# Branch B's scores: four products over 128 rows become six over 64 rows

## The chip, the cores and the metric

The kernel runs on one core of one Trainium2 chip. The metric is the device time of one execution in microseconds. The runs before the change took 1885.35, 1890.58 and 1890.80 us (median 1890.58). A profile is one execution, recorded instruction by instruction. Its engines are TensorE (PE; its weight loads are shown apart as PEld), VectorE (DVE), ScalarE (ACT), GpSimd (POOL) and SyncE (SP), which issues the DMA transfers.

## The reference

One layer of a bidirectional encoder is applied to 2048 prompt tokens and to 512 sample tokens, each with 16 learned meta tokens ahead. After a normalisation, one wide projection gives the operands of two attention branches, their gates, and two merge gates. Branch A is attention in a two-dimensional neighbourhood. Branch B, which the change touches, is attention in a sliding window:

```python
s_band = einsum('bnqkgd,bnckd->bnkgqc', qr, k_band) * scale + band_bias   # 128 queries, up to 3 blocks of 128 keys
s_band = where(visible, s_band, NEG_INF)
s_meta = einsum('bnqkgd,bmkd->bnkgqm', qr, km) * scale + meta_bias        # 16 meta keys
p = softmax(concatenate([s_band, s_meta, sink_col], -1), -1)
o = p[band] @ v_band + p[meta] @ v_meta
```

It has 8 query heads of width 64 and 2 key/value heads; four query heads share a key head. The branches' outputs are gated, projected, merged, projected again and added to the input, and a last normalisation follows. All inputs and outputs are 32-bit floats.

## The kernel before

The tokens are cut into 5 windows of 512 (`w`; window 0 is the sample). A first part computes all projections and writes queries, keys, values and gates to DRAM. A second part, from about 980 us on, runs the attention and the dense projections of the merge, window by window, first the units of branch A and then those of branch B.

**High and low parts.** TensorE takes its operands in a single-pass 32-bit type. To keep accuracy, an operand is split into a high part, rounded to that type, and a low part, the rest. A product of two split operands is made of part products.

**A unit of branch B** (`unit_b`) is one block of 128 queries (`n`, 4 in a window) for a pair of query heads (`p = 2 * gh + i`; `gh` is the key head). There are 5 x 2 x 4 x 2 = 80 units. Its keys are 18 columns of meta keys, sink and padding (`EXTRA`) and two or three blocks of 128, so a row of scores has 274 or 402 columns (`ncol`). The steps of a unit are:

1. load queries, keys, values, bias and gate (SP);
2. the scores of the two heads, each in a PSUM bank of the pool `ps_s`, which has two; VectorE adds the bias and takes the maximum (`scores_max`, L1042), ScalarE takes the exponential (`exps`, L1049);
3. normalise the probabilities;
4. transpose them on TensorE (L1237, L1240) and split them (L1244, L1245);
5. multiply with the values (L1261, L1264, L1266) and add into the output.

**Scores before.** A head is 64 wide and TensorE contracts over 128 rows. The tile of queries of a head has 128 rows: for each of the 64 features the high and the low part of the query, one below the other. The tile of keys `kbt` has the same 128 rows with the key's part repeated: once the high part in both rows, once the low part. So one product gives (high + low query) by high key, a second (L1218) adds (high + low query) by low key: all four part products in two products of 128 rows a head, four in a unit. To have the rows so arranged, the key is written to DRAM twice (`put_k`, one copy for each `j`) and read with feature and copy interleaved; the query is read with feature and part interleaved.

**The order of the work.** On TensorE the order is written out: the loop at the end of the attention steps through the units, with a unit's transposes while the next unit's scores are already made, and between the steps it calls `fill`, which issues pieces of the dense projections (L146, L147, L148: the three part products of `mm3`). In the projections SP's order is written out too; in the attention the order of SP, VectorE, ScalarE and GpSimd is set by a planner from its own cost estimates. A step waits on semaphores for its operands and for its buffers.

The lines that matter: L1217 and L1218 are the score products; L1111 and L1112 those of branch A; L185 and L361, early in the kernel, belong to the normalisation of the meta tokens (`spread` and `prep_last`) and work on 16 tokens: L185 has a product over 16 rows, L361 one with 16 columns; L142 is `move`, by which nearly all DMAs are issued.

Of the kernel before, what the change touches and what calls it, by code (L numbers as in the profile page):

```python
# [9 lines left out]
F32 = mybir.dt.float32  # L10
# [7 lines left out]
P = 128  # L18
D_MODEL = 1024
KT = D_MODEL // P  # L20
N_META = 16
# [3 lines left out]
TOK = SEQ + DEC_SEQ  # L25
WTOK = 512
# [6 lines left out]
EXTRA = N_META + 2  # L33
# [62 lines left out]
def encoder_block(ctx: ExitStack, tc: tile.TileContext, xT, x_end, w_in, w_pa, w_pb, w_o, norm_g, final_g,  # L96
                  final_row, bias_a0, bias_a1, bias_a2, bias_a3, bias_b, bias_b0, outT_p, outT_s, out_e):
    nc = tc.nc
# [4 lines left out]
    def dt(name, shape):  # L103
        return dram.tile(shape, F32, tag=name, name=name)

    qa_d = {(w, p): dt(f"qa{w}{p}", [P, 2, 2 * WTOK]) for w in range(NWIN) for p in range(4)}
    qb_d = {(w, p): dt(f"qb{w}{p}", [P, 2, WTOK]) for w in range(NWIN) for p in range(4)}
    ka_d = [dt(f"ka{p}", [P, 2, TOK]) for p in range(4)]
    kam_d = [dt(f"kam{p}", [P, 2, GRID_W]) for p in range(4)]
    kb_d = dt("kb", [P, 2, 2, TOK])  # L110
    kbm_d = dt("kbm", [P, 2, 2, EXTRA])
    va_d = [dt(f"va{p}", [2, TOK // GRID_W * 8, 8, P]) for p in range(4)]
    va0_d = [dt(f"va0{p}", [2, P, 6, P]) for p in range(4)]
    vrow_d = [dt(f"vrow{p}", [8, 8, 2, P]) for p in range(4)]
# [7 lines left out]
    def f32(ap):  # L122
        return ap.bitcast(F32)
# [17 lines left out]
    def move(out, in_):  # L141
        last_move[0] = nc.sync.dma_start(*(f32(a) if a.dtype == F32R else a for a in (out, in_)))  # L142
        return last_move[0]
# [73 lines left out]
    class Weights:  # L217
# [12 lines left out]
        def split(self, i):  # L230
            if i < len(self.srcs):
                self.wt[i] = split_w(self.raw.pop(i))
# [377 lines left out]
    def put_k(br, w, p, src):  # L610
        e = ev.tile([P, 2, WTOK], F32R, tag="ev", name="evk")
        split(e[:, 0, :], e[:, 1, :], src, 0.125)
        ws = slice(w * WTOK, (w + 1) * WTOK)
        if br == "a":
            move(ka_d[p][:, :, ws], e)
        else:
            for j in range(2):
                move(kb_d[:, j, :, ws], e)

    km = st.tile([P, 2, GRID_W], F32R, tag="km", name="km", bufs=1)  # L620

    def put_k_meta(br, p, src):
        c0, n = (META_COLS[0], len(META_COLS)) if br == "a" else (0, 1)
        if p == 0:
            nc.vector.memset(f32(km), 0.0)
        hi, lo = (km[:, i, c0 : c0 + n * N_META].rearrange("p (n m) -> p n m", m=N_META) for i in range(2))
        split(hi, lo, src[:, None, :].broadcast_to([P, n, N_META]), 0.125)
        if br == "a":
            move(kam_d[p], km)
        else:  # L630
            for j in range(2):
                move(kbm_d[:, j], km[:, :, :EXTRA])

    def transposed(dst, src, nch, n):

# [97 lines left out]
    def put_kv(f, w, src):  # L733
        if f < VA:
            put_k("a", w, f - KA, src)
        elif f < ZA:
            put_values("a", w, f - VA, src)
        elif f == KB:
            put_k("b", w, 0, src)
        else:  # L740
            put_values("b", w, 0, src)
# [23 lines left out]
    def alone(f, wt, held):  # L765
# [27 lines left out]
        if f in (*range(KA, VA), KB):  # L793
            put_k_meta(br, p, tm)
        else:
            later(lag[0], put_v_meta, br, p, tm)
# [242 lines left out]
    def scores_max(s, n, bias):  # L1039

        nm = at.tile([P, 1], F32, tag="nm", name="nm", bufs=8)
        nc.vector.tensor_tensor_reduce(s[:, :n], s[:, :n], bias, -1.0, 3.0e38, ALU.add, ALU.min, nm)  # L1042
        return nm

    def sums_of():
        return at.tile([P, 2], F32, tag="sm", name="sm", bufs=8)

    def exps(out, s, nm, sm):
        nc.scalar.activation(out, s, AF.Exp, bias=nm, scale=-1.0, accum_out=sm)  # L1049
# [115 lines left out]
    def unit_b(w, gh, n, i, sh):  # L1165
# [1 line left out]
        kinds = [b_blocks(w, m) for m in range(4)]  # L1167
        tlo = kinds[0][0]
        thi = kinds[3][0] + kinds[3][1] * P
        gs = slice(64 * gh, 64 * gh + 64)  # L1170
        p = 2 * gh + i
        b0, nbk, first = kinds[n]
        ncol = EXTRA + nbk * P
        qs = slice(n * P, (n + 1) * P)
# [3 lines left out]
        if n == 0 and i == 0:  # L1178
            q = sh["q"] = ld.tile([P, 2, 2, WTOK], F32R, tag="q", name="q")
            for j in range(2):  # L1180
                move(q[:, j], qb_d[w, p + j].rearrange("(h d) i t -> (d i) h t", h=2))
            bt = sh["b"] = ld.tile([P, 2, 2, EXTRA + 3 * P + N_META], F32, tag="ba", name="bb")
            for j in range(2):
                move(bt[:, j, :, : EXTRA + 3 * P], bias_b[p + j])
                move(bt[:, j, 0, EXTRA + 3 * P :], bias_b[p + j][:, 0, :N_META])
# [6 lines left out]
            move(z, z_d["b", w, p])  # L1192
        if i == 0:
            kt = sh["k"] = ld.tile([P, 2, EXTRA + 3 * P + N_META], F32R, tag="kd", name="kbt")
            move(kt[:, :, EXTRA : EXTRA + nbk * P],
                 kb_d[gs].rearrange("d j i t -> (d j) i t")[:, :, b0 : b0 + nbk * P])
            move(kt[:, :, :EXTRA], kbm_d[gs].rearrange("d j i t -> (d j) i t"))
            move(kt[:, :, ncol : ncol + N_META], kbm_d[gs].rearrange("d j i t -> (d j) i t")[:, :, :N_META])
        kt, q, z = sh["k"], sh["q"][:, i], sh.get(("z", i))
        yield  # L1200
        if n == 0:
# [6 lines left out]
        if nbk == 2 and not first:  # L1208
            nc.vector.tensor_copy(bt[:, 0, ncol : ncol + N_META], bt[:, 0, :N_META])
        sm = sums_of()  # L1210
        for h in range(2):
            if h and (gh, n, i) == (0, 0, 0):
                yield
            s = ps_s.tile([P, WTOK], F32, tag="s", name="s")

            ks = slice(N_META * (1 - h), N_META * (1 - h) + ncol)
            nc.tensor.matmul(s[:, :ncol], q[:, h, qs], kt[:, 0, ks], start=True, stop=False)  # L1217
            nc.tensor.matmul(s[:, :ncol], q[:, h, qs], kt[:, 1, ks], start=False, stop=True)  # L1218
            nm = scores_max(s, ncol, bt[:, h, ks])
            exps(prs[:, cols[h]], s[:, :ncol], nm, sm[:, h : h + 1])  # L1220
        yield
# [37 lines left out]
        for m, (j, hi, lo) in enumerate(parts):  # L1259
            vb = sh["v"][:, (b0 - tlo) // P + j, :]  # L1260
            nc.tensor.matmul(o[:, : 2 * P], vb, hi, start=(m == 0), stop=False, skip_group_check=True)  # L1261
            if m == nbk - 1:
                for h in range(2):
                    nc.tensor.matmul(o[:64, h * P : (h + 1) * P], vms[:, gh, h, :], pms[(2 * n + i) % 2], start=False,  # L1264
                                     stop=False, skip_group_check=True)
# [3 lines left out]
        for h in range(2):  # L1269
            hs = slice(64 * h, 64 * h + 64)  # L1270
# [232 lines left out]
    for w in range(NWIN):  # L1503
        for p in range(4):
            sh = {}
            units += [("a", w, unit_a(w, p, h, g, sh), 1) for h in range(2) for g in range(4)]
        for gh in range(2):
            sh = {}
            units += [("b", w, unit_b(w, gh, n, i, sh), 2) for n in range(4) for i in range(2)]
# [13 lines left out]
    ps_s = ctx.enter_context(tc.tile_pool(name="ps_s", bufs=2, space=PSUM))  # L1523
# [10 lines left out]
    with tc.manual_schedule(engines={E.PE}):  # L1534
# [22 lines left out]
        for i in range(N):  # L1557
            br, w, _, weight = units[i]
# [128 lines left out]
```

## Time and profile before

| | |
|---|---|
| runs, median (lowest to highest) | 1890.58 us (1885.35 to 1890.80) |
| profiled span, first to last instruction | 1881.7 us |
| median of the runs less the span | 8.9 us |
| TensorE busy | 1855.9 us, 9797 products, as many weight loads |
| VectorE, ScalarE, GpSimd busy | 1320.6, 1145.5, 730.0 us |
| mean granted TensorE clock | 0.999 |
| DMA, mean rate | 226 GB/s |
| branch B's score products | 320: 256 of 402 columns, 64 of 274 |

The profiled execution's own time outside the profiler is not known; beside its span of 1881.7 us stand the runs. In a row of the timeline the numbers are start and duration in us, then the engine, the line of the kernel, the operation, the tile written and the tiles read, and the shape: `128*64 128x256` is a product over 128 rows with 64 stationary columns and 256 moving ones. Products are pipelined, so the duration of one is longer than the distance to the next. In a row of the groups stand the busy time, the mean duration in ns, and the idle time before with what ended it.

### The profile page before, as it was taken

Reading aid. Unit: us, or ns where it says so; the run is one execution under the profiler, and the core shown is the slowest. Engines: PE = TensorE matmul, PEld = TensorE weight load, DVE = VectorE, ACT = ScalarE, POOL = GpSimd, SP = SyncE. Lnnn points to the kernel's source line nnn. Section 1 sums busy time; section 2 is a strip of 40 time slices with the busy share of each in tenths; the row PEclk is TensorE's granted clock in tenths of the full one; section 3 lists DMA queues with packets and bytes.
Section 4 is the critical chain, followed back from the end, with each engine's and each line's share of the span. In section 5 each row is a group of like instructions: output and inputs, shape, how many; then the busy total and the mean of one; then the engine's idle time right before and its main releaser. Section 6 shows DMA issues by size and latency. Waiting matters only on the chain. (4 is left out here: it accounts for less than half of the span.)

```text
span 1881.7 us, 29782 instructions
## 1 busy us (share of the span) xinstructions
PE 1855.9 (99%) x9797; PEld 1583.0 (84%) x9797; DVE 1320.6 (70%) x2961; ACT 1145.5 (61%) x2528; POOL 730.0 (39%) x558
## 2 busy tenths in 40 slices
PE   8999999999999999999999999999999999999998
PEld 6898888888888888888888888888888888888887
DVE  8886657556477565444457888878787887888874
ACT  6454444444365443444456797797789788878932
POOL 2005443323202233322324435656744763685420
PEclk9999999999999999999999999999999999999999
DMA  7667756544296777744258878977985996798383
GB/s 268 234 175 295 207 171 193 211 175 179 84 348 219 235 216 200 209 138 161 104 197 310 273 217 266 304 213 249 316 280 179 320 315 225 222 311 260 119 299 135
DMA packets 290385, 424.83 MB, mean 226 GB/s; under 512 B 117416, under 2 KB 162040, under 8 KB 288696
## 3 DMA queue, kind: packets, MB, share of 16 engines
q1 hardware_dynamic: 289944, 422.93, 69.5%
q8 instruction: 78, 1.28, 0.3%
q14 instruction: 75, 0.61, 0.1%
q10 hardware_dynamic: 288, 0.01, 0.0%
HBM read 303.46 MB, written 119.39 MB: 225 GB/s over the span
## 5 line engine op out<-in xcount | busy, mean ns | idle before, releaser
L208 POOL TENSOR_TENSOR wt<-wraw,wt 128x512 fp32r<-128x512 f32 x164 | 213.1, 1318 | 265.9 <-ACT wt L207 265.8
L848 PE MATMUL pa<-u,wt 128*128 128x512 f32 x1008 | 242.5, 389 | 0.0
L848 PE MATMUL pa<-u,x 128*128 128x512 f32 x984 | 236.9, 390 | 1.2 <-ACT u L859 1.1
L207 ACT CAST wt<-wraw 128x512 fp32r<-128x512 f32 x312 | 177.9, 619 | 74.8 <-PE mm L148 35.3
L848 PEld LDWEIGHTS pa<-u,wt 128*128 128x128 f32 x1008 | 189.0, 188 | 39.2
L848 PEld LDWEIGHTS pa<-u,x 128*128 128x128 f32 x984 | 184.3, 188 | 40.6 <-ACT u L859 2.2
L819 POOL TENSOR_TENSOR s<-wraw,raw 128x512 f32<-128x512 f32 x40 | 58.3, 1458 | 265.5 <-DVE x L208 265.5
L146 PE MATMUL mm<-u,wt 128*128 128x512 f32 (+2 forms) x416 | 150.4, 362 | 7.8 <-ACT u L334 7.2
L814 POOL TENSOR_TENSOR s<-raw 128x512 f32<-128x512 f32 x40 | 58.3, 1456 | 250.0 <-DMA raw<-in_w_in_dram 245.0
L148 PE MATMUL mm<-u,wt 128*128 128x512 f32 (+2 forms) x416 | 146.6, 352 | 2.4 <-DVE wt L208 2.4
L147 PE MATMUL mm<-u,wt 128*128 128x512 f32 (+2 forms) x416 | 146.6, 352 | 1.3 <-DVE u L335 1.3
L208 DVE TENSOR_TENSOR wt<-wraw,wt 128x512 fp32r<-128x512 f32 x148 | 107.2, 762 | 47.2 <-ACT wt L207 47.0
L848 PE MATMUL pe<-u,wt 128*128 128x512 f32 x504 | 121.3, 390 | 0.0
L848 PE MATMUL pc<-u,wt 128*128 128x512 f32 x504 | 121.1, 389 | 0.0
L848 PE MATMUL pe<-u,x 128*128 128x512 f32 x480 | 115.3, 389 | 0.0
L848 PEld LDWEIGHTS pc<-u,wt 128*128 128x128 f32 x504 | 94.6, 188 | 19.6
L848 PEld LDWEIGHTS pe<-u,wt 128*128 128x128 f32 x504 | 94.4, 188 | 19.6
L1139 DVE TENSOR_TENSOR pl<-tp,ph 128x384 fp32r<-128x384 f32 (+6 forms) x160 | 94.8, 593 | 20.2 <-ACT ph L1138 17.7
L1138 ACT CAST ph<-tp 128x384 fp32r<-128x384 f32 (+6 forms) x160 | 81.7, 510 | 43.4 <-PE tp L1135 41.9
L146 PE MATMUL pso<-mh,wt 128*128 128x512 f32 x256 | 107.1, 418 | 0.0
L827 POOL TENSOR_TENSOR s<-wraw,s 128x512 f32<-128x512 f32 x40 | 55.4, 1384 | 131.6 <-DVE wt L208 126.3
L848 PEld LDWEIGHTS pe<-u,x 128*128 128x128 f32 x480 | 90.1, 188 | 18.7
(258 smaller groups left out, 5017.0 us busy)
## 6 DMA issues: line engine op xcount, KB each, us to landing
wraw<-in_w_in_dram SPq DMA_DIRECT2D x86, 512.0 KB
qa<-evq SPq DMA_DIRECT2D x20, 1024.0 KB
raw<-in_w_in_dram SPq DMA_DIRECT2D x40, 512.0 KB
q<-qa SPq DMA_DIRECT2D x20, 1024.0 KB
wraw<-in_w_o_dram SPq DMA_DIRECT2D x32, 512.0 KB
kbt<-kb SPq DMA_DIRECT2D x32, 384.0 KB
qb<-evq SPq DMA_DIRECT2D x20, 512.0 KB
ka<-evk SPq DMA_DIRECT2D x20, 512.0 KB
```

The costliest lines, as they stand in the source:

```text
L146: nc.tensor.matmul(ps, wh, uh, start=first, stop=False)
L147: nc.tensor.matmul(ps, wh, ul, start=False, stop=False)
L148: nc.tensor.matmul(ps, wl, uh, start=False, stop=last)
L207: nc.scalar.copy(h, r)
L208: low[0] = (eng or lo_eng[0]).tensor_sub(l, r, f32(h)).ins
L814: eng.tensor_add(s1, a21, a22)
L819: eng.tensor_sub(s3, a11, a21)
L827: eng.tensor_sub(s4, a12, s2)
L848: nc.tensor.matmul(ps, wt[:, a, s], u[:, b, kk, :], start=first and kk == 0 and i == 0, stop=kk == 3 and i == 2, skip_group_check=True)
L1138: nc.scalar.copy(ph_[:kb, a], tb)
L1139: nc.vector.tensor_sub(pl_[:kb, a], tb, f32(ph_[:kb, a]))
```

## The change

Head 0 of a pair takes rows 0 to 63 of TensorE's array, head 1 rows 64 to 127. The query tile's 128 rows are now the two heads' 64 features; its high and low parts lie side by side along the free axis (`q[hs, iq, qs]`). The key tile has the same key head in both halves, its high and low part side by side (`kt[hs, ik, ...]`). For each head there are three products of 64 rows: high query by high key, high by low, low by high; the product of the two low parts is dropped. The two heads' products alternate, and both score banks are taken before the first. The keys are written to DRAM into a tensor for each key head, into both halves of its 128 rows, with four transfers where there were two (the meta keys likewise); queries and keys are read back without interleaving.

```diff
-    kb_d = dt("kb", [P, 2, 2, TOK])
-    kbm_d = dt("kbm", [P, 2, 2, EXTRA])
+    kb_d = [dt(f"kb{g}", [P, 2, TOK]) for g in range(2)]
+    kbm_d = [dt(f"kbm{g}", [P, 2, EXTRA]) for g in range(2)]
...
-            for j in range(2):
-                move(kb_d[:, j, :, ws], e)
+            for g, j in (0, 0), (0, 1), (1, 0), (1, 1):
+                move(kb_d[g][64 * j : 64 * j + 64, :, ws], e[64 * g : 64 * g + 64])
...
-            for j in range(2):
-                move(kbm_d[:, j], km[:, :, :EXTRA])
+            for g, j in (0, 0), (0, 1), (1, 0), (1, 1):
+                move(kbm_d[g][64 * j : 64 * j + 64], km[64 * g : 64 * g + 64, :, :EXTRA])
...
-                move(q[:, j], qb_d[w, p + j].rearrange("(h d) i t -> (d i) h t", h=2))
+                move(q[:, j], qb_d[w, p + j])
...
-            move(kt[:, :, EXTRA : EXTRA + nbk * P],
-                 kb_d[gs].rearrange("d j i t -> (d j) i t")[:, :, b0 : b0 + nbk * P])
-            move(kt[:, :, :EXTRA], kbm_d[gs].rearrange("d j i t -> (d j) i t"))
-            move(kt[:, :, ncol : ncol + N_META], kbm_d[gs].rearrange("d j i t -> (d j) i t")[:, :, :N_META])
+            move(kt[:, :, EXTRA : ncol], kb_d[gh][:, :, b0 : b0 + nbk * P])
+            move(kt[:, :, :EXTRA], kbm_d[gh])
+            move(kt[:, :, ncol : ncol + N_META], kbm_d[gh][:, :, :N_META])
...
         sm = sums_of()
+        kss = [slice(N_META * (1 - h), N_META * (1 - h) + ncol) for h in range(2)]
+        ss = [ps_s.tile([P, WTOK], F32, tag="s", name="s") for _ in range(2)]
+        for m, (iq, ik) in enumerate(((0, 0), (0, 1), (1, 0))):
+            for h in range(2):
+                hs = slice(64 * h, 64 * h + 64)
+                nc.tensor.matmul(ss[h][:, :ncol], q[hs, iq, qs], kt[hs, ik, kss[h]], start=m == 0, stop=m == 2)
+        if (gh, n, i) == (0, 0, 0):
+            yield
         for h in range(2):
-            if h and (gh, n, i) == (0, 0, 0):
-                yield
-            s = ps_s.tile([P, WTOK], F32, tag="s", name="s")
-
-            ks = slice(N_META * (1 - h), N_META * (1 - h) + ncol)
-            nc.tensor.matmul(s[:, :ncol], q[:, h, qs], kt[:, 0, ks], start=True, stop=False)
-            nc.tensor.matmul(s[:, :ncol], q[:, h, qs], kt[:, 1, ks], start=False, stop=True)
+            s, ks = ss[h], kss[h]
             nm = scores_max(s, ncol, bt[:, h, ks])
             exps(prs[:, cols[h]], s[:, :ncol], nm, sm[:, h : h + 1])
```

More of the change, by code (lines that the diff above doesn't have):

```diff
@@ L1169, in unit_b @@
         thi = kinds[3][0] + kinds[3][1] * P
-        gs = slice(64 * gh, 64 * gh + 64)
         p = 2 * gh + i
```

## The prediction

> **What bounds the kernel now.** I read the page first (busy time, slices), then the busy time by stage, then TensorE's timeline around a unit of branch B.
>
> ```profile
> PE 1855.9 (99%) x9797; PEld 1583.0 (84%) x9797; DVE 1320.6 (70%) x2961; ACT 1145.5 (61%) x2528; POOL 730.0 (39%) x558
> ...
> PE   8999999999999999999999999999999999999998
> ...
> 1380.00:1460.00 80.00, 79.71 (x485) 70.72 (x484) 65.39 (x194) 72.21 (x186) 37.63 (x29) 1.00 0.67 210
> 1460.00:1540.00 80.00, 79.44 (x482) 68.81 (x481) 64.85 (x166) 61.18 (x139) 60.33 (x48) 1.00 1.01 317
> ```
>
> The last two rows are two 80 us stages: the first holds the 16 B units of a window, the second A units. The columns are PE, PEld, DVE, ACT, POOL, then the granted clock (1.00), the DMA share and GB/s. TensorE has 0.29 us without work in a whole B stage; ACT is next with 72.21 of 80. A busy PE may still be PE waiting inside its pipeline, so the test is the spacing of its products (timeline: start, duration, engine, line):
>
> ```profile
> 1398.22 0.28 PE L1264 MATMUL ob<-pms,vms 96*64 96x128 f32 x2
> 1398.34 0.28 PE L1266 MATMUL ob<-pl,vb 128*64 128x256 f32 x1
> 1398.46 0.35 PE L1217 MATMUL s<-kbt,q 128*128 128x402 f32 x1
> 1398.64 0.34 PE L1218 MATMUL s<-kbt,q 128*128 128x402 f32 x1
> 1398.83 0.35 PE L1217 MATMUL s<-kbt,q 128*128 128x402 f32 x1
> 1399.01 0.35 PE L1218 MATMUL s<-kbt,q 128*128 128x402 f32 x1
> 1399.20 0.39 PE L146 MATMUL pso<-mh,wt 128*128 128x512 f32 x1
> 1399.42 0.39 PE L147 MATMUL pso<-ml,wt 128*128 128x512 f32 x1
> ```
>
> A duration (0.35 us) is a product's passage through the array; the price is the distance between starts. The unit's four score products take 1399.20 - 1398.46 = 0.74 us, 0.185 us each, and 512 columns take about 0.23 us: both near 2.2 columns a nanosecond, with no gap on either side. So TensorE's stream sets the end here, and what the change adds to or takes from this stream is worth its full length. Units with 274 columns:
>
> ```profile
> 1783.38 0.29 PE L1217 MATMUL s<-kbt,q 128*128 128x274 f32 x1
> 1783.51 0.30 PE L1218 MATMUL s<-kbt,q 128*128 128x274 f32 x1
> 1783.64 0.29 PE L1217 MATMUL s<-kbt,q 128*128 128x274 f32 x1
> 1783.77 0.29 PE L1218 MATMUL s<-kbt,q 128*128 128x274 f32 x1
> 1783.90 0.39 PE L146 MATMUL psa<-ya,wt 128*128 128x512 f32 x1
> ...
> L1217 PE MATMUL s<-kbt,q 128*128 128x402 f32 x128 | 44.6, 348 | 0.0
> L1217 PE MATMUL s<-kbt,q 128*128 128x274 f32 x32 | 9.3, 301 | 0.6 <-ACT prs L1049 0.6
> ```
>
> Here a product costs 0.52 / 4 = 0.13 us. L1217 runs twice a unit, so 128 / 2 = 64 units have 402 columns and 16 have 274: 80 units.
>
> **The change, part by part.**
>
> *The products.* Four products of 128 rows become six of 64 rows: for each of three parts (high by high, high by low, low by high; low by low is dropped), head 0 in rows 0 to 63 and head 1 in rows 64 to 127, into two PSUM banks. No row of this trace has two products on disjoint rows; every product shares rows with its neighbour, and they stream one after the other. So the cost has two ends. If the two heads of a part stream together, a unit takes three rounds: 3 x 0.185 = 0.555 us, 0.185 us less than now (0.13 us less at 274 columns): 64 x 0.185 + 16 x 0.13 = 13.9 us gained. If they stream one after the other, it takes six: 2 x 0.185 = 0.37 us more (0.26 at 274): 64 x 0.37 + 16 x 0.26 = 27.8 us lost. I take the first end: what makes neighbours queue in every row above is that they want the same rows of the array, and these two share neither rows nor bank.
>
> The Trainium skill, "TensorE: Matmul & The Clock Gate", Part 3 (packing small matmuls), says that products on distinct row groups run concurrently, and gives 3.07 times for four of 32 rows; no run here shows it. By it the products alone would gain the 13.9 us.
>
> *Stagger.* Six weight loads replace four. A load of the second head queues behind the first's; the two 96-row products of L1264 lie (1398.34 - 1398.22) / 2 = 0.06 us apart, loads included. So head 1 starts up to 0.06 us after head 0 and ends as much later: 0 to 0.06 us a unit, and I take 0.06, since a load cannot be skipped. Later loads have a round of 0.185 us for two, and hide.
>
> *Switching the array's division.* Before and after each unit's scores TensorE runs products over 128 rows. Weight loads (PEld) normally start far ahead. Two places early in the kernel show what a switch to fewer rows or columns does, and back:
>
> ```profile
> 22.86 0.70 PE L360 MATMUL fin_v<-ones,rs 128*128 128x1 f32 x5
> 23.49 0.11 PEld L361 LDWEIGHTS fin_v<-ones,rs 128*16 128x16 f32 x2
> 23.49 0.20 PE L361 MATMUL fin_v<-ones,rs 128*16 128x1 f32 x2
> 23.62 0.19 PEld L146 LDWEIGHTS mm<-u,wt 128*128 128x128 f32 x1
> ...
> 31.54 0.29 PEld L185 LDWEIGHTS rs_rb<-rs_dg,ones 16*128 16x128 f32 x2
> 31.54 0.39 PE L185 MATMUL rs_rb<-rs_dg,ones 16*128 16x16 f32 x2
> 31.86 0.19 PEld L146 LDWEIGHTS mm<-u,wt 128*128 128x128 f32 x1
> 31.86 0.50 PE L146 MATMUL mm<-u,wt 128*128 128x512 f32 x1
> 32.20 0.40 PE L147 MATMUL mm<-u,wt 128*128 128x512 f32 x1
> ```
>
> The 16-row products end at 31.54 + 0.39 = 31.93, and the load of the next, 128-row product starts only at 31.86, 0.07 us before. The same 0.07 us stands at 23.49 (before 22.86 + 0.70 = 23.56) and at 23.62 (before 23.69): the load waits until the array is nearly empty. The product behind it ends at 32.36, 0.43 us after the one before, where 512 columns normally end 0.23 us after (L147 ends at 32.60): a switch costs 0.20 us. Against it stand 64-column products:
>
> ```profile
> 1398.28 0.14 PEld L1266 LDWEIGHTS ob<-pl,vb 128*64 128x64 f32 x1
> 1398.34 0.19 PEld L1217 LDWEIGHTS s<-kbt,q 128*128 128x128 f32 x1
> ...
> L1266 PE MATMUL ob<-pl,vb 128*64 128x256 f32 x224 | 60.0, 281 | 0.0
> ```
>
> L1266's product runs from 1398.34 to 1398.62, and the load of the 128-column product after it starts at 1398.34, 0.28 us before that end: no emptying. So a switch costs between 0 (64 columns) and 0.20 us (16 rows, 16 columns). For 64 rows I take 0.20: the change divides the rows, and the one row-divided place, on the way out, pays it in full. Two switches a unit: 0.40 us, 80 x 0.40 = 32.0 us.
>
> The Trainium skill, "TensorEngine Tiling (Array Packing)", Key Properties, says that changing the tiling mode, not just the tile, drains the array. The trace agrees at 16 rows and columns and shows no drain at 64 columns; by the rule without exception the switches cost the 32.0 us, by the 64-column row nothing.
>
> *Order within the unit.* Both score banks must now be free before the second product, not before the third, and head 0's scores are complete later. The chain behind the scores of 1398.46, and the next unit's:
>
> ```profile
> 1399.02 0.58 DVE L1042 CUSTOM_DVE_ANT_0 s<-s,bb 128x402 f32<-128x402 f32 x1 [0.53 <-PE s L1218]
> 1401.80 0.59 ACT L1049 ACTIVATE prs<-s,nm 128x402 f32<-128x402 f32 x1
> 1403.55 0.35 PE L1217 MATMUL s<-kbt,q 128*128 128x402 f32 x1
> ```
>
> Head 0's maximum starts at 1399.02; head 1's exponential, which frees the second bank, ends at 1401.80 + 0.59 = 1402.39, and the next scores start at 1403.55. The second bank was needed two products later, 1.5 us after that end; now 1.16 us. Head 0's scores come some 0.2 to 0.6 us later, and this slack hides it: 0. Without that cover each unit would wait for ACT, as once already (0.6 us, in the row of L1217 above). Behind a waiting score product stands the dense fill; there is no other new wait.
>
> *DMAs.* Keys go out in four transfers a window instead of two (10 more in all), the meta keys in four instead of two; loads keep their number and bytes, a query row becoming one run instead of two.
>
> ```profile
> L142 SPq DMA_DIRECT2D kb<-evk x10: 382/456/472, 127.1 to 758.3; - x10
> ```
>
> Twelve issues of 0.456 us are 5.5 us of SP spread over the projections; the keys written last at 758.3 are read by B units after 1060. Hidden: 0.
>
> *Sum.* At 402 columns: -0.185 + 0.06 + 0.40 = +0.275 us; at 274: -0.13 + 0.06 + 0.40 = +0.33 us. 64 x 0.275 + 16 x 0.33 = 17.6 + 5.3 = 22.9 us longer. The profiled span is 1881.7 us, so 1904.6 us; the median of the runs, 1890.58 us, lies 8.9 us above the span (the runs spread by 5.5 us), which gives **1913.5 us**.
>
> **The rivals.**
>
> *Pairs together, switches free* (the other side). The array runs 64-row tiles as it runs 64-column ones: loads go ahead, three rounds follow with no gap. Place: the two edges of each unit's scores. Price: -13.9 us to -13.9 + 80 x 0.06 = -9.1 us; 1876.7 to 1881.5, about 1878 us. For it: every row of size 64 in the trace, and these are of the same number type as the scores; against it: the 16-row rows, the only ones with divided rows. It decides as soon as a switch costs less than (13.9 - 4.8) / 160 = 0.057 us.
>
> *One after the other.* The heads don't overlap. With free switches +27.8 us: 1918.4 us; with drained ones +27.8 + 32.0 = +59.8 us: 1950 us. For it: no two products in the trace overlap in the array. Against it: none could have. This is also the case in which the change does not do what it says.
>
> *A cheaper switch.* If a switch costs about half (0.10 us), the sum is -9.1 + 16.0 = +6.9 us without other luck, and about +2 us with no stagger: 1893 to 1898 us. For it: nothing but the middle between the two bounds.
>
> *ACT takes over.* In the B stage ACT is busy 72.21 of 80 us; with 2.2 to 2.8 us less of TensorE per stage it would reach 93%. It would blunt the gain of the first rival, not turn it; I count it in its range.
>
> **How the numbers follow.** Together and drained (forecast, 1913): 0.42, its own range 1906 to 1917. Together and free (1878): 0.36, range 1876 to 1883. In series, free (1918): 0.08. In series and drained (1950): 0.07. Cheaper switch (1893 to 1898): 0.07. About 0.3% (5.7 us) is what a measurement of this kernel tells from no change. Faster: 0.36 and a little of the last, 0.37; same: 0.06; slower: 0.42 + 0.08 + 0.07, 0.57. The range must reach from the free case to the drained one: 1876 to 1919; it leaves out the fully drained series.
>
> **What would show it.** The number of TensorE products rises by 160 to 9957 in every case. Together: the two heads' products of one part start less than 0.1 us apart and parts 0.185 us apart; in series: six starts 0.185 us apart. Drained: the first weight load of a unit's scores, and the first load after them, start 0.07 us before the end of the product before; free: 0.28 us or more before. The stage of 16 B units lengthens by 16 x 0.275 = 4.4 us if I am right, and shortens by 2 to 3 us if the first rival is. I am wrong if loads at the switch run ahead as in L1266, or if the time moves outside the B stages by more than 3 us.

## The result and the profile after

The kernel after takes 1919.18 us (median of 4 runs, 1918.28 to 1921.56) against 1889.49 us before (one more run of the kernel before, of 1888.40 us, has moved its median). The ratio is 1.0169, 95% interval 1.0152 to 1.0185: slower by 28.7 to 35.0 us. The forecast was slower, at about 1913 us in a range of 1876 to 1919; the time lies 0.2 us above the range and 6 us above the forecast. The span of after's profile lies 1.9 us below its own execution's time (1919.7 against 1921.56). By that, some 7 of the 8.9 us that the prediction put around the span of 1881.7 us mean that its profile was of a quick execution.

First the switch and the pairs. The timeline of TensorE in one unit after (start, duration, engine, line):

```profile
1422.64 0.28 PE L1266 MATMUL ob<-pl,vb 128*64 128x256 f32 x1
1422.86 0.82 PE L1214 MATMUL s<-kbt,q 64*128 64x402 f32 x6
1423.61 0.50 PE L146 MATMUL pso<-mh,wt 128*128 128x512 f32 x1
```

Its weight loads in the same stretch:

```profile
1422.86 0.48 PEld L1214 LDWEIGHTS s<-kbt,q 64*128 64x128 f32 x6
1423.61 0.19 PEld L146 LDWEIGHTS pso<-mh,wt 128*128 128x128 f32 x1 [0.27 <-issue]
```

Six products of 402 columns are through in 0.82 us: one passage of 0.45 us and two more rounds of 0.185 us. Six in a row would need five more, 1.37 us. The ends of products are modelled in the trace, but the starts are recorded, and L146 starts 0.75 us after the first of the six, which is less than six rounds of 0.185 us (1.11 us). So the pairs stream together. The first score load starts at 1422.86, 0.06 us before the end of L1266 (1422.64 + 0.28 = 1422.92); the load after the scores starts at 1423.61, 0.07 us before the scores' end (1422.86 + 0.82 = 1423.68). At both edges the load waits until the array is nearly empty, as at the 16-row place of before.

From the end of the product before the scores to the end of the 512-column product after them it is 1423.61 + 0.50 - 1422.92 = 1.19 us here; before, 1399.20 + 0.39 - (1398.34 + 0.28) = 0.97 us. Over all units with such neighbours the medians of this distance, taken from the product ends in the trace, are 0.964 us before and 1.178 us after at 402 columns, 0.746 and 1.012 us at 274. That gives 64 x 0.214 + 16 x 0.266 = 18.0 us.

The second part of the loss lies ahead of the first changed product. The weight loads of branch A's first score product, grouped by line, first before and then after (behind the count the shortest, median and longest in ns, then the starts of the first and the last):

```profile
L1111 PEld LDWEIGHTS s<-kd,q x160: 186/188/192, 981.5 to 1712.2; 128*128 128x128 f32 x160
```

```profile
L1111 PEld LDWEIGHTS s<-kd,q x160: 186/188/330, 991.0 to 1746.7; 128*128 128x128 f32 x160
```

The projections end 9.5 us later, before any 64-row product has run. The issues of the key stores on SP after, in a row of the same form:

```profile
L142 SPq DMA_DIRECT2D kb<-evk x20: 514/644/1243, 129.5 to 769.2; - x20
```

The median issue takes 0.644 us (0.456 before), and there are twice as many: over the five windows the key stores hold SP for 15.0 us where it was 4.4. Among TensorE's waits after in the first 981 us, this is the row for ScalarE's copies (sum, number, longest):

```profile
PE pa L848 <- ACT u L859: 5.1, 4, 2.3
```

TensorE stood four times for them, 5.1 us in all.

Third, the clock. Busy time by stage after, the columns as in the prediction (PE, PEld, DVE, ACT, POOL, granted clock, DMA share, GB/s):

```profile
1294.00:1298.00 4.00, 2.75 (x19) 2.19 (x17) 3.92 (x12) 3.75 (x10) 1.62 (x2) 1.00 0.69 194
1298.40:1301.60 3.20, 3.20 (x10) 2.63 (x11) 2.46 (x13) 1.12 (x4) 0.00 (x0) 0.50 0.59 195
1302.00:1306.00 4.00, 4.00 (x27) 3.14 (x26) 3.20 (x13) 2.29 (x7) 0.07 (x1) 1.00 0.02 6
```

And TensorE's timeline at the beginning of the second row:

```profile
1297.37 1.02 PE L170 MATMUL fin_v<-ones,ssq 128*128 128x1 f32 x8 [1.25 <-DVE pms L1255]
1298.25 0.73 PE L146 MATMUL psa<-ya,wt 128*128 128x512 f32 x1
1298.78 0.63 PE L147 MATMUL psa<-ya,wt 128*128 128x512 f32 x1
```

After TensorE stood for 1.25 us, the granted clock is 0.50 for some 3.4 us, and products of 512 columns pass in 0.63 us instead of 0.39. Half speed for 3.4 us costs about 1.7 us, an estimate. The profile of after shows three such stretches in the attention (from 1298.3, 1380.2 and 1649.9); the profile of before shows none there, nor does the second profile of before below. The other two come behind stands of 2.07 us (at 1379.0) and 1.05 us (at 1647.6). But a stand of 1.05 us at 1474.9 has none behind it, nor has one of 1.82 us in the second profile of before, so the length of one stand alone does not decide it.

The Trainium skill, "TensorE: Matmul & The Clock Gate", gives windows of some 3.4 us, and half rate after at least one idle window (section "What's actually happening"). Half rate and length agree with these rows; the idle window does not, since the stands ahead of the three stretches were shorter, 1.05 to 2.07 us.

### The profile page after: what moved, and what is told of

Its sections match the earlier page's. It is cut to its first block, busy times and chain, and to the rows that moved or that the text cites. A ratio compares the mean times of both kernels' runs of the same rounds, so it can differ in the third digit from the quotient of the medians.

```text
span 1919.7 us, 30120 instructions
## 1 busy us (share of the span) xinstructions
PE 1883.1 (98%) x9957; PEld 1573.8 (82%) x9957; DVE 1323.2 (69%) x2961; ACT 1142.6 (60%) x2528; POOL 725.5 (38%) x558
## 3 DMA queue, kind: packets, MB, share of 16 engines
q8 instruction: 79, 1.29, 0.3%
## 4 chain that ended last, share of the span: by engine, by line
PE 46%; ACT 5%; DMA 4%; DVE 3%; issue 1%; POOL 0%; SPq 0%; DVEq 0%; ACTq 0%
PE pa L848 6%; PE pe L848 3%; PE tp L1135 3%; PE pso L146 2%; PE pso L148 2%; PE pso L147 2%; PE s L1214 2%; DMA sgb<-gb 2%; PE psa L146 2%; PE tp L1237 2%; PE psa L148 2%; PE pc L848 2%; PE psa L147 2%; PE psb L148 2%; PE psb L147 1%; PE psb L146 1%
## 5 line engine op out<-in xcount | busy, mean ns | idle before, releaser
L848 PE MATMUL pa<-u,wt 128*128 128x512 f32 x1008 | 243.1, 390 | 0.6 <-ACT s L859 0.4
L848 PE MATMUL pa<-u,x 128*128 128x512 f32 x984 | 237.2, 390 | 5.1 <-ACT u L859 5.1
L848 PEld LDWEIGHTS pa<-u,wt 128*128 128x128 f32 x1008 | 188.7, 188 | 41.0 <-ACT s L859 0.8
L848 PEld LDWEIGHTS pa<-u,x 128*128 128x128 f32 x984 | 184.3, 188 | 45.1 <-ACT u L859 6.8
L146 PE MATMUL mm<-u,wt 128*128 128x512 f32 (+2 forms) x416 | 151.8, 365 | 7.8 <-ACT u L334 7.2
L848 PE MATMUL pe<-u,wt 128*128 128x512 f32 x504 | 121.3, 390 | 0.0
L848 PE MATMUL pc<-u,wt 128*128 128x512 f32 x504 | 121.1, 389 | 0.0
L848 PE MATMUL pe<-u,x 128*128 128x512 f32 x480 | 115.3, 389 | 0.0
L1049 ACT ACTIVATE prs<-s,nm 128x402 f32<-128x402 f32 (+1 forms) x160 | 90.9, 571 | 40.7 <-DVE nm L1042 39.8
L146 PE MATMUL pso<-mh,wt 128*128 128x512 f32 x256 | 112.4, 439 | 0.0
L848 PEld LDWEIGHTS pc<-u,wt 128*128 128x128 f32 x504 | 94.6, 188 | 19.6
L848 PEld LDWEIGHTS pe<-u,wt 128*128 128x128 f32 x504 | 94.5, 188 | 19.6
L1042 DVE CUSTOM_DVE_ANT_0 s<-s,ba 128x384 f32<-128x384 f32 (+5 forms) x160 | 86.7, 543 | 28.3 <-PE s L1112 26.5
```

The costliest lines, as they stand in the source:

```text
L146: nc.tensor.matmul(ps, wh, uh, start=first, stop=False)
L848: nc.tensor.matmul(ps, wt[:, a, s], u[:, b, kk, :], start=first and kk == 0 and i == 0, stop=kk == 3 and i == 2, skip_group_check=True)
```

## The experiments

**The kernel before again, for a second profile** (no edit).

> The kernel before, unchanged, for a second profile. Its first profile shows a span of 1881.7 us and the first branch-A scores at 981.5 us; the kernel after shows 1919.7 us and 991.0 us, so 9.4 us of the 38.0 us between the two spans lie ahead of the first changed product. Theory 1 (those 9.4 us are scatter between executions and not the change): this profile differs from the first of the same kernel by several us too, with the first scores between 982 and 990 us. Theory 2 (the new layout of the keys costs them): the first scores come at 981 to 983 us again.

1888.28 us, ratio 0.9991 (0.9978 to 1.0005), span 1885.7 us. The loads of branch A's first score product here:

```profile
L1111 PEld LDWEIGHTS s<-kd,q x160: 186/188/192, 982.7 to 1716.3; 128*128 128x128 f32 x160
```

And TensorE's wait for ScalarE's copies in the first 981 us:

```profile
PE pa L848 <- ACT u L859: 0.7, 1, 0.7
```

The first branch-A scores come at 982.7 us, where theory 2 put them. So the 991.0 us of after are unlikely to be scatter, though part of the distance between the two spans (4 of 38 us) was the quick first profile. Theory 2 stands so far: the new layout or its transfers cost the first part.

**The layout without the 64-row products.** The kernel after with four products over 128 rows; it leaves out the telling apart of the two heads:

```diff
-        for m, (iq, ik) in enumerate(((0, 0), (0, 1), (1, 0))):
-            for h in range(2):
-                nc.tensor.matmul(ss[h][:, :ncol], q[hs, iq, qs], kt[hs, ik, kss[h]], start=m == 0, stop=m == 2)
+        for h in range(2):
+            for m in range(2):
+                nc.tensor.matmul(ss[h][:, :ncol], q[:, m, qs], kt[:, m, kss[h]], start=m == 0, stop=m == 1)
```

> The kernel after with its layout of queries and keys and all its transfers, but with four products over 128 rows as before (two a head, both banks taken first). Left out: the two heads are not told apart, each score is the sum over both heads, high by high plus low by low; the amount of work from there on is the same. Theory 1 (the loss is the change of the array's division before and after each unit's scores, and nothing comes from layout and transfers): 1886 to 1895 us, the time of before. Theory 2 (the layout costs the 9.4 us of the first part): 1897 to 1903 us.

1892.97 us, ratio 1.0024 (1.0011 to 1.0037): 4.5 us slower than before. The time lies inside theory 1's range, but its interval excludes no change, which theory 1 meant; and it lies below theory 2's range, though the first branch-A scores come late, at 989.7 us. The units of B take 0.964 us as before. From the first branch-A scores to the end it is 1891.0 - 989.7 = 901.3 us, no more than in the second profile of before (1885.7 - 982.7 = 903.0); after needs 1919.7 - 991.0 = 928.7 us. So layout, transfers and the two banks taken first cost 2 to 7 us together, and the larger part of after's loss, all of it in the attention, comes with the 64-row products.

**The products ordered by head** instead of by part:

```diff
-        for m, (iq, ik) in enumerate(((0, 0), (0, 1), (1, 0))):
-            for h in range(2):
-                hs = slice(64 * h, 64 * h + 64)
+        for h in range(2):
+            hs = slice(64 * h, 64 * h + 64)
+            for m, (iq, ik) in enumerate(((0, 0), (0, 1), (1, 0))):
```

> The kernel after with the six 64-row products ordered by head: three of head 0, then three of head 1. Theory 1 (the two heads of a part stream together, so six products take three rounds): products of one head queue on the same rows, only the last of head 0 and the first of head 1 overlap, five rounds: 2 x 0.185 us at 64 units and 2 x 0.13 us at 16 more, +27.8 us, about 1947 us. Rival (the starts are recorded together but the products share the stream, so order is of no account): 1919 us.

1918.71 us, ratio 1.0155 (1.0126 to 1.0184): no difference from after. The expectation of five rounds (1947 us) fell. The rival had the time right, but the trace does not bear out its reason, a shared stream. The timeline of one unit:

```profile
1412.53 0.28 PE L1152 MATMUL oa<-pl,v 128*64 128x256 f32 x1
1412.74 0.82 PE L1214 MATMUL s<-kbt,q 64*128 64x402 f32 x6
1413.50 0.50 PE L146 MATMUL pso<-mh,wt 128*128 128x512 f32 x1
```

Six products are through in 0.82 us again, and L146 starts 0.76 us after the first of them. They do overlap, although head 0's three stand ahead of head 1's first: TensorE started head 1's first product, fourth in the order, 0.01 us after head 0's first (median over the units). The record does not name the head. But only a head's first product waits for a bank, and in 64 of the 80 units the first two to start, and no others, are those that wait for a semaphore. Each half of the array took its own products in turn.

**Two more switches a unit, and the same small product without a switch.** In the kernel after, 16 columns into unread columns of head 0's bank after the first round:

```diff
         for m, (iq, ik) in enumerate(((0, 0), (0, 1), (1, 0))):
+            if m == 1:
+                nc.tensor.matmul(ss[0][:, 480:496], q[:, 0, qs], kt[:, 0, :N_META], start=True, stop=True,
+                                 skip_group_check=True)
```

The other run has `q[:64, 0, qs], kt[:64, 0, :N_META]`. In both, the small product starts anew in head 0's bank between its parts, and so changes head 0's scores; the amount of work is the same.

> The kernel after with one more small product (16 columns) over 128 rows after the first round of each unit, into columns of the bank that nobody reads: two more changes of the array's division a unit, 160 in all. Theory 1 (each change costs 0.20 us): +32 us and some 0.03 to 0.06 us a unit for the product itself, 1951 to 1957 us. Rival (the gaps at the edges of a unit are waits for operands or banks, not the division): at most 5 us more, 1919 to 1924 us.

> The kernel after with the same small product as in the run with two more changes, but over 64 rows, so that the division stays as it is through the unit. Theory 1 (the change of division is what costs): 0 to 0.06 us a unit, 1919 to 1924 us. Rival (any product put between the rounds breaks the pairs and costs): +0.2 us a unit or more, 1935 us or more.

1942.24 us (ratio 1.0273, 1.0245 to 1.0300) and 1925.77 us (1.0194, 1.0164 to 1.0223). In the next two fences L1217 is the scores' product, L1213 the added one and L1269 the product before the unit (L1266 in after). With the switches:

```profile
1433.51 0.28 PE L1269 MATMUL ob<-pl,vb 128*64 128x256 f32 x1
1433.72 0.45 PE L1217 MATMUL s<-kbt,q 64*128 64x402 f32 x2
1434.11 0.28 PE L1213 MATMUL s<-kbt,q 128*128 128x16 f32 x1
1434.31 0.63 PE L1217 MATMUL s<-kbt,q 64*128 64x402 f32 x4
1434.87 0.50 PE L146 MATMUL pso<-mh,wt 128*128 128x512 f32 x1
```

Without:

```profile
1429.74 0.28 PE L1269 MATMUL ob<-pl,vb 128*64 128x256 f32 x1
1429.95 0.45 PE L1217 MATMUL s<-kbt,q 64*128 64x402 f32 x2
1430.25 0.17 PE L1213 MATMUL s<-kbt,q 64*128 64x16 f32 x1
1430.25 0.63 PE L1217 MATMUL s<-kbt,q 64*128 64x402 f32 x4
1430.81 0.50 PE L146 MATMUL pso<-mh,wt 128*128 128x512 f32 x1
```

From the end of L1269 to the end of L146 it is 1.58 us with the switches and 1.29 us without (medians 1.585 and 1.280), against 1.178 us in after. The small product itself costs 0.10 us (up to 0.06 was expected), the two switches 0.30 us more; together 0.41 us, where 0.43 to 0.46 was expected. So around a short product a switch costs 0.15 us, not 0.20. The time rose by 23 us against after, not by 32 to 38, and so lies between the ranges of theory 1 and of the rival. The trace shows why the units' 0.41 us do not all appear: the run with the switches has no stretch of half clock in its attention (some 5 us in after), and the waits at L1135 and L170, 7.3 us in after, are 0.4 us here. The control came out 1.8 us above theory 1's range and 9 us below the rival's. Both runs add the same small product at the same place; only the switches differ. So the gap at a unit's edges is the switch and not a wait for operands or banks.

**The order alone.** The kernel before with both banks taken first and the 128-row products alternating between the heads:

```diff
+        ss = [ps_s.tile([P, WTOK], F32, tag="s", name="s") for _ in range(2)]
+        for m in range(2):
+            for h in range(2):
+                nc.tensor.matmul(ss[h][:, :ncol], q[:, h, qs], kt[:, m, kss[h]], start=m == 0, stop=m == 1)
...
-            nc.tensor.matmul(s[:, :ncol], q[:, h, qs], kt[:, 0, ks], start=True, stop=False)
-            nc.tensor.matmul(s[:, :ncol], q[:, h, qs], kt[:, 1, ks], start=False, stop=True)
```

> The kernel before with the order of after and nothing else: both score banks are taken first and the products alternate between the heads; layout and the four 128-row products stay. Theory 1: the slack of 1.2 us behind the banks hides it, 1886 to 1895 us. Rival (the part of the loss that the changes of division do not explain, some 10 us, is the wait for both banks and the later scores of head 0): 1896 to 1903 us.

1890.47 us, ratio 1.0017 (1.0006 to 1.0029): 1 to 5 us slower than the kernel before, run beside it. That is inside theory 1's range and below the rival's, but it is not nothing.

**Which divisions need a switch.** The kernel before with one small product between the two heads of each unit:

```diff
+            if h == 0:
+                r, c = ((P, P), (64, P), (32, P), (P, 64), (P, 32))[w]
+                nc.tensor.matmul(s[:c, 480:496], q[:r, 0, n * P : n * P + c], kt[:r, 0, :N_META], start=True, stop=True,
+                                 skip_group_check=True)
```

> The kernel before with one small product (16 columns, into unread columns of the bank) between the scores of the two heads of each unit of B, of another shape in each window: 128 rows and 128 columns in window 0, 64 rows in 1, 32 rows in 2, 64 stationary columns in 3, 32 stationary columns in 4. The unit's time in the timeline tells what a change of division costs. Theory 1: 64 rows, 32 rows and 32 columns cost 0.40 us a unit (two changes), 128 x 128 and 64 columns 0.06 us or less; in all 3 x 16 x 0.40 = 19 us and up to 5 us for the products, 1908 to 1914 us. Rival (only a division into rows empties the array, and the 32-column place early in the kernel was late for another reason): window 4 costs nothing, 1902 to 1907 us.

1906.22 us, in one execution only: below theory 1's range (1908 to 1914) and inside the rival's (1902 to 1907). The units of the trace decide. L1221 is the small product. Units with 64 rows, 32 rows and 32 columns:

```profile
1256.25 0.35 PE L1217 MATMUL s<-kbt,q 128*128 128x402 f32 x1
1256.71 0.27 PE L1221 MATMUL s<-kbt,q 64*128 64x16 f32 x1
1257.39 0.40 PE L146 MATMUL pso<-mh,wt 128*128 128x512 f32 x1
...
1417.74 0.35 PE L1217 MATMUL s<-kbt,q 128*128 128x402 f32 x1
1418.20 0.27 PE L1221 MATMUL s<-kbt,q 32*128 32x16 f32 x1
1418.88 0.39 PE L146 MATMUL pso<-mh,wt 128*128 128x512 f32 x1
...
1754.36 0.35 PE L1217 MATMUL s<-kbt,q 128*128 128x402 f32 x1
1754.73 0.17 PE L1221 MATMUL s<-kbt,q 128*32 128x16 f32 x1
1755.21 0.39 PE L146 MATMUL pso<-mh,wt 128*128 128x512 f32 x1
```

From the start of the first score product to that of L146 it is 1.14 us at 64 and at 32 rows, 0.85 us at 32 columns, and 0.74 us in the kernel before. The medians of the time that the small product adds at 402 columns are 0.109 us for 128 x 128, 0.108 for 64 columns, 0.114 for 32 columns, 0.407 for 64 rows and 0.400 for 32 rows. The rival holds: of these shapes, only the divisions into rows cost a switch. Why the loads at 23.49 and 23.62 us, at the 16-column product of the profile before, waited is open; that product is of the full 32-bit type and not of the scores' type, and no run tries this.

**Four key stores instead of two**, in the kernel before, to the same places:

```diff
-            for j in range(2):
-                move(kb_d[:, j, :, ws], e)
+            for g, j in (0, 0), (0, 1), (1, 0), (1, 1):
+                move(kb_d[64 * g : 64 * g + 64, j, :, ws], e[64 * g : 64 * g + 64])
```

> The kernel before with one edit: each window's keys go to DRAM in four transfers of 64 rows instead of two of 128 rows, the same bytes to the same places; everything else, the four 128-row products too, as before. In the run with the layout alone these transfers hold SP for 3.2 us a window instead of 0.9 us, and what queues behind them on SP (stores that free buffers) is late. Theory 3 (this is what the first part loses in the kernel after): the first branch-A scores come 6 to 8 us later than in the two profiles of before (981.5 and 982.7 us), at 988 to 991 us, and the time rises by 3 to 7 us, 1892 to 1896 us. Rival (the reads of the new layout, or a planner's order that only the new layout brings): 981 to 985 us and no change in the time.

1896.25 us, ratio 1.0051 (1.0038 to 1.0063): 9.5 us slower, more than expected. SP's queue at one window's stores, in the second profile of before:

```profile
311.73 0.90 SPq L142 DMA_DIRECT2D kb<-evk  x2
312.72 0.83 SPq L142 DMA_DIRECT2D wraw<-in_w_in_dram  x1
313.60 1.18 SPq L142 DMA_DIRECT2D raw<-in_w_in_dram  x1
314.87 0.99 SPq L142 DMA_DIRECT2D xa<-in_xT_dram  x2
```

In this run:

```profile
315.80 3.25 SPq L142 DMA_DIRECT2D kb<-evk  x4
319.15 1.12 SPq L142 DMA_DIRECT2D wraw<-in_w_in_dram  x1
320.32 1.15 SPq L142 DMA_DIRECT2D raw<-in_w_in_dram  x1
321.56 1.02 SPq L142 DMA_DIRECT2D xa<-in_xT_dram  x2
```

And on TensorE in this run:

```profile
337.66 3.74 PE L848 MATMUL pa<-u,x 128*128 128x512 f32 x10 [1.98 <-ACT u L859]
```

Four issues hold SP for 3.25 us where two held it 0.90. The loads behind them are issued later relative to the stores: that of `xa` starts 5.8 us after the first store instead of 3.1. What comes of it can be followed. VectorE needs `xa` at L377, first in the second profile of before:

```profile
321.15 3.47 DVE L377 SCALAR_TENSOR_TENSOR xa<-xa,ng,rsa 128x512 f32<-128x512 f32 x4 [2.51 <-DMA xa<-in_xT_dram]
```

In this run, with ScalarE's copy `u` behind it:

```profile
328.39 3.54 DVE L377 SCALAR_TENSOR_TENSOR xa<-xa,ng,rsa 128x512 f32<-128x512 f32 x4 [6.53 <-DMA xa<-in_xT_dram]
337.04 0.57 ACT L859 COPY u<-pa 128x512 f32<-128x512 f32 x1
```

VectorE waits 6.53 us for `xa` instead of 2.51. ScalarE waits for the work behind that on VectorE (2.19 us at L293) and makes the copy `u` late, and TensorE stands 1.98 us for that copy at L848, as in after. The first branch-A scores come at 993.2 us. So the stores suffice for the loss of the first part; the new layout isn't needed for it. Not all of the lateness is waiting: this profile has about 6.8 us more at half clock in the first part than the second profile of before (3.4 of them right behind the stand, from 338.7), some 3.4 us lost, an estimate.

**Two key stores in the kernel after**, of 128 rows into two copies; keys read with one transfer from both copies, or with two of 64 rows. With one read:

```diff
-    kb_d = [dt(f"kb{g}", [P, 2, TOK]) for g in range(2)]
+    kb_d = dt("kb", [2, P, 2, TOK])
...
-            for g, j in (0, 0), (0, 1), (1, 0), (1, 1):
-                move(kb_d[g][64 * j : 64 * j + 64, :, ws], e[64 * g : 64 * g + 64])
+            for j in range(2):
+                move(kb_d[j, :, :, ws], e)
...
-            move(kt[:, :, EXTRA : ncol], kb_d[gh][:, :, b0 : b0 + nbk * P])
...
+            gs = slice(64 * gh, 64 * gh + 64)
+            move(kt[:, :, EXTRA : ncol], kb_d[:, gs, :, b0 : b0 + nbk * P])
...
```

With two reads, in place of the last line:

```diff
+            for j in range(2):
+                js = slice(64 * j, 64 * j + 64)
+                move(kt[js, :, EXTRA : ncol], kb_d[j, gs, :, b0 : b0 + nbk * P])
...
```

> The kernel after with the keys written in two transfers of 128 rows a window, as before the change, into two copies in DRAM, from which the key tile of a unit is read with one transfer (64 rows of each copy); the 64-row products as in after. Theory 3 (the four 64-row stores on SP are the part of the loss that lies in the projections): the first branch-A scores come at 981 to 985 us instead of 991.0, the time falls by 4 to 7 us against after, 1912 to 1915 us; what is left against before, 23 to 26 us, is 18 us of switches less rounds and stalls in the attention. Rival: 1917 to 1921 us, as after.

> As the run with two key stores a window, the 64-row products as in after, but each read of keys is two transfers of 64 rows (one for each copy) instead of one transfer with two outer steps, whose issues held SP for some 5.5 us each in that run. Theory 3 (the four 64-row stores are the loss in the projections): the first branch-A scores come at 981 to 985 us as in that run, and 1912 to 1915 us in all, 4 to 7 us less than after, if the 120 more issues of reads hide in the attention. Rival (the issues of reads cost as much as the stores did): 1917 us or more.

With one read from both copies: 2121.91 us, ratio 1.1247 (1.1232 to 1.1262). The first part is mended (scores from 983.9 us), but the reads became slow:

```profile
L142 SPq DMA_DIRECT2D kbt<-kbm x80: 494/5504/8151, 1062.5 to 2004.1; - x80
```

TensorE's waits for them (sum, number, longest):

```profile
PE s L1215 <- DMA kbt<-kbm: 151.0, 31, 9.0
```

An issue of 16 or 18 columns of meta keys holds SP for 5.5 us (0.6 before), and TensorE waits 151 us for them. So the run says nothing on the stores' share of the time. It isn't every read from two copies that holds SP: the main read of the keys, ahead of the two of meta keys, does not. On SP, and then the busy time of the engines while SP is held (columns as above):

```profile
1071.16 0.51 SPq L142 DMA_DIRECT2D kbt<-kb  x1
1071.72 12.23 SPq L142 DMA_DIRECT2D kbt<-kbm  x2
```

```profile
1076.00:1080.00 4.00, 2.08 (x13) 1.56 (x10) 1.63 (x4) 2.56 (x6) 1.61 (x2) 1.00 0.13 50
```

In these 4 us the DMA share is 0.13, as much as two of the 16 DMA engines make, and 50 GB/s move. That fits transfers from two copies that occupy few DMA engines, so that what is issued behind them has to wait. The run with two reads fits this too, with 0.6 us an issue, but no run tests the number of engines. With two reads of 64 rows the first scores' loads:

```profile
L1111 PEld LDWEIGHTS s<-kd,q x160: 186/188/192, 983.5 to 1738.4; 128*128 128x128 f32 x160
```

The first part is as before (983.5 us), as theory 3 has it. The profiled span is 1911.3 us, 8.4 us less than after's; some 5 us of that are the three stretches of half clock, which this profile doesn't have. But the median of its runs is 1918.41 us (1913.23 to 1921.08; ratio 1.0164, 1.0146 to 1.0181), no better than after and in the rival's range. Its runs at a mean clock of 0.998, 0.997, 0.996 and 0.995 took 1913, 1915, 1919, and 1918 and 1921 us. From the first branch-A scores to the end its profile needs 927.7 us; after's 928.7 us are some 923.6 without half clock. So the attention lost about 4 us of what the first part gained, and TensorE has waits for the meta keys in it (1.4 us in all) that after's profile doesn't show. The 7.5 us that the first part gains are seen in the trace; in the time they are not shown, and the rival, that the added reads cost as much, is not excluded.

## Why the prediction came out as it did

**Three rounds instead of six: right.** Pairs stream together, and the third round starts 0.184 us after the second (medians of the starts). The medians of the whole distance fit a gain of 0.185 us a unit together with the switches below; the two were not measured apart.

**The switch: right, and its size too.** With 0.779 us for three rounds and the product behind (0.964 - 0.185), after's 1.178 us leave 0.40 us for two switches, the 0.40 taken. The size rested on one place with 16 rows, so that it came out to the hundredth is partly luck: around a short product it is 0.15 us a switch and not 0.20. The 16-row place was the row to go by. The 16-column place was not: columns cost nothing at 64 or at 32 in the scores' type. The rule of the Trainium skill, "TensorEngine Tiling (Array Packing)", Key Properties, that a change of mode drains the array, holds in these runs for rows and not for 64 or 32 columns.

**The stagger: wrong.** I took 0.06 us because a second load could not be skipped. In 74 of the 80 units after, the two heads' first products start at most 0.004 us apart; the term is nil. Without it the sum is 18.1 us, against 18.0 us measured. The 4.8 us too much stood by luck against the losses left out: without them the forecast would have been some 1909 us, 10 us off instead of 6.

**The DMAs: the step that failed.** I multiplied twelve issues by the old duration, 0.456 us, and wrote "Hidden: 0" because the keys are read much later. The issue of a 64-row store costs more (0.64 us median, 3.2 us for four in place of 0.9 for two), and what mattered was not the reader of the keys but what stands behind the stores on SP: loads that VectorE, ScalarE and at last TensorE wait for. The first branch-A scores came 8.3 to 9.5 us later, ahead of every changed product. This is the prediction's own sign of being wrong, time that moves outside the B stages by more than 3 us. In the kernel before, the four stores alone cost 7 to 12 us of the time; with the new layout and both banks taken first the loss was 2 to 7 us. The Trainium skill has a rule that speaks against this step, "DMA: Bandwidth & Descriptors", Rules for kernel authors: for two disjoint halves of the partitions, use one transfer over all of them. The SP rows above agree: 0.90 us for two issues of 128 rows, 3.25 us for four of 64. What these rows show is time on the issuing queue.

**The order: 0 was taken, 1 to 5 us measured** with 128-row products.

**The clock was not in the sum.** After's runs have a mean clock of 0.996, the runs of before beside its second profile 0.997 to 0.999; 0.002 of 1919 us is about 4 us, an estimate.

Between the second profile of before and the profile of after lie 1919.7 - 1885.7 = 34.0 us. Of these, 8.3 us (991.0 - 982.7) stand ahead of the first branch-A scores and 25.7 us behind them. Of the 25.7 us, 18.0 are switches less rounds and about 5 the three stretches of half clock; some 3 us are left, as much as the waits ahead of L170 grew (3.3 us in after, 0.5 before). In the time, 18.0 us and the 4.5 us of the layout run leave some 7 us of the 29.7 us between the medians, to which clock and waits can add up; these shares overlap and weren't separated. Nor is it shown why the waits ahead of L170 grew: the order in which the planner put the work of VectorE and ScalarE differs between the two kernels.

The likeliest case was the one that came: together and drained. What pushed the time out of the range was the terms set to nothing, the DMAs above all, and the clock that the sum did not have.

## What to carry to other kernels

Here the 64-row pairs cut four rounds to three but paid about 0.4 us for going to rows and back. So they pay only when enough work stands between two switches: at 0.185 us saved a unit, three units' scores would have to share one stay on 64 rows. That is an estimate from these numbers, and no run tries it. Count the instructions that a change adds to a queue with what stands behind them, not with who reads their data. And see that the rows of the trace from which a price comes have the same number type and the same operand side as the work they are to price.

## What the runs showed of the hardware

- Products on different rows of the array did not wait for their place in the program: with three products of head 0 ahead, head 1's first started 0.01 us after head 0's first (median), and six took 0.82 us in either order.
- A stay on fewer rows cost 0.30 us with a short product in it and 0.40 us around long ones; 64 and 32 rows cost nearly the same (0.407 and 0.400 us with the product); 64 and 32 columns cost no more than the product itself (0.108 and 0.114 us, against 0.109).
- Behind a read of keys from two copies in DRAM, SP was held 5.5 us by an issue of meta keys (median), while the DMA share was 0.13; with each copy read by itself such an issue took 0.6 us.
- Four stores of 64 rows held SP for 3.2 us, two of 128 rows for 0.9 us, with the same bytes.
